# Streaming encoder layer: six first gate products ahead in block one, their order against the first product with t, two more rooms for sums of weights, and the first weight splits behind the columns

## The chip, the core and the metric

The kernel runs on one core of one Trainium2 chip. The core has five engines that each run their own list of instructions strictly in order: TensorE (PE, with its weight loads shown as PEld), VectorE (DVE), ScalarE (ACT), GpSimd (POOL) and SyncE (SP), which only issues transfers here. The metric is device microseconds of one execution; lower is better.

## The reference, cut to what matters

One layer of a streaming encoder on 2048 prompt rows and 64 sample rows, width 1024. The part around the change is the end of the mixers and the feed-forward:

```
x = x + gt1 * (merged @ p['w_o'])
h2 = rms_norm(x, p['norm2_g']) * (1 + sc2) + sh2
gate, up = jnp.split(h2 @ p['w_ffn_in'], 2, axis=-1)
x = x + gt2 * ((jax.nn.silu(gate) * up) @ p['w_ffn_out'])
```

`w_ffn_in` is 1024 x 5632 (2816 gate columns, 2816 up columns), `w_ffn_out` 2816 x 1024, all in f32.

## The kernel before

**Products.** An f32 product is made from three matmuls on halves of the mantissa: each operand is split into a high part (`hi`, a copy on ACT into the type F32R) and a low part (`lo`, source minus high part, on DVE or POOL), and `mm3` adds hi*hi, hi*lo and lo*hi. A split of weights gives a slab `whi`, `wlo`; five slabs are held, and a sixth split waits until TensorE is through with the oldest.

**Blocks.** After attention the tokens are taken in three blocks (`CBLOCKS`): 576, 768 and 768 rows. For each block `s` the kernel merges the mixers, multiplies by `w_o` (tiles `pw`), adds the residual and normalises by tiles of 128 rows (`residual`), turns the rows into columns by transposes on TensorE, and runs the feed-forward. The text calls the block with `s = 0` block one; half of its tokens are 288, so a feed-forward matmul there has 288 columns.

**Seven products instead of eight.** The up part of the feed-forward works on a pair of a gate column and an up column of 128 (`f` from 0 to 21), on two halves of the tokens and two halves of the 1024 inputs. It uses sums of weights, `s1 = u0 + u1`, `s2 = s1 - g0`, `s3 = g0 - u0`, `s4 = g1 - s2` (`Weights.operand`, on POOL, into tiles `ws`, four rooms), and sums of activations, `t1` to `t4`, which `residual` makes on DVE and ACT from the columns `b11`, `b21` (first half of the tokens) and `b12`, `b22` (second half). One product is 12 matmuls: four pieces of 128 inputs, three matmuls each. `up(f)` makes `s3*t3`, `s2*t2`, `s1*t1`, `a22*t4`, `s4*b22`, and the gate's own `a11*b11`, `a12*b21`.

**Products ahead.** `b11` and `b21` need only the first half of the tokens, so they are there before the last token tiles have their columns. For the first `EARLY = 5` gates, `first(f)` (`a11*b11`) and `second(f)` (`a12*b21`, then tanh on ACT and a step on DVE, `silu`) run ahead of `up(0)` and leave both results in tiles `early`. Their weights are whole gate columns with the key `("fi", f * P)`; a split with an odd `f` puts its low part on DVE, with an even one on POOL. The results of one product lie in a PSUM bank; the names `y0`, `z0`, `y1`, `z1` are one bank each. In the last rows of a block the tile before the last (called the fourth token tile in the text, of five in block one) keeps its columns and their sums in `y1` and `z1`; the fifth has other banks.

**Order.** The program hands out instructions with a planner (`Stream`) that adds up an estimated load for each engine, and runs the steps of `residual` as generators (`turns`) between products; a low part of an `up` or `fo` weight goes to DVE if the planned load of POOL is more than `POOL_BEHIND` = 3000 ns ahead of TensorE's. A scheduler then fixes each engine's list: of the instructions that it reckons ready, the one handed out first. `tc.issue_after(ins)` keeps the instructions of its block behind `ins` on the same engine's list. In block one `W.hold` keeps sums and splits of the up weights back until all columns have been handed out. Then come `W.presum()`, which hands out the sums for `f = 0`, `W.begin_last()`, the rest of `turns`, and the products `first(3)`, `second(2)`, `first(4)`, `second(3)`, `second(4)`.

**Rooms and queues.** Raw weights are loaded by SP into rooms `wst` (three), `wup` (one) and `wfo` (two), in the order of `weight_order`; in block one raw columns are shared by all keys that need them (`Weights.first`), and sums go out to DRAM (`sum_d`) for blocks two and three. `token_row` hands out six rooms for whole rows (`x1`, `xn`, later the results `acc`); five of them become `acc` in block one.

## Time and profile before

| | |
|---|---|
| median of 3 runs | 2994.05 us (2993.24 to 2994.75) |
| profiled execution | 2994.99 us, span of the trace 2993.2 us |
| mean granted TensorE clock | 0.995 |
| TensorE busy | 2912.7 us, 97% of the span |
| VectorE, ScalarE, GpSimd busy | 2024.7, 1355.1, 1141.4 us |
| HBM read, written | 476.53 MB, 148.54 MB |
| chain of waits, by engine | PE 80%, DVE 8%, DMA 4%, ACT 2%, POOL 2%, issue 2% |

All lines of the kernel carry one line number (L102, the helper that records every operation), so instructions are told apart by their tiles: `ps<-b` is a product with `b11`, `b21` or `b22`, `ps<-t` one with `t1` to `t4`, `pd` one of the down part, `pw` a bank with the rows of `w_o` or, later, with columns of the last tiles, `xn` the other half of those columns. A row of a timeline has the start in us from the start of the span, the length, engine, operation, result and sources, and in brackets the idle time ahead of it on that engine with what ended it; a row with x3 stands for three instructions in a row. Block one's feed-forward begins near 1312 us, block two's near 1866, block three's near 2495.

### The profile page before, as it was taken

The page shows a single profiled execution, that of the slowest core. Times are in us where ns is not written, and L with a number is a line of the kernel's source. Part 1 is how long each engine was busy: PE and PEld are TensorE (multiplying, and loading weights), DVE is VectorE, ACT ScalarE, POOL GpSimd, SP SyncE. Part 2 cuts the span into 40 slices and gives each one's busy share as a digit, 9 for nine tenths or more (in the row PEclk, how much of TensorE's full clock was granted, in tenths as well). Part 3 has the DMA queues.
Part 4 walks back from the last instruction along what each step waited for, and adds up shares of the span by engine and source line. Part 5 has one row for each costly group of instructions (what it writes and reads, how often), then busy time and mean ns, then how long its engine had stood idle before and what let it go on. Part 6 is the DMA issues. An engine that isn't in the chain of part 4 may idle for free.

```text
span 2993.2 us, 44914 instructions
## 1 busy us (share of the span) xinstructions
PE 2912.7 (97%) x16259; PEld 2593.7 (87%) x16259; DVE 2024.7 (68%) x3596; ACT 1355.1 (45%) x2437; POOL 1141.4 (38%) x734
## 2 busy tenths in 40 slices
PE   7999899999999999989999999999999999999999
PEld 4899777787888788888989889999999999999998
DVE  5887687767857885477677755666666657466666
ACT  3335643662456257464444335534444345344442
POOL 0201310111011102354566433256666741466667
PEclk9999999999999999999999999999999999999999
DMA  8889889888987789885444786423333975333333
GB/s 290 289 284 304 266 288 314 282 255 275 308 280 221 275 246 286 254 293 166 141 141 152 232 269 216 138 89 115 118 101 115 307 248 183 96 93 116 116 102 127
DMA packets 467724, 628.06 MB, mean 210 GB/s; under 512 B 36276, under 2 KB 314664, under 8 KB 467501
## 3 DMA queue, kind: packets, MB, share of 16 engines
q1 hardware_dynamic: 453456, 605.58, 62.5%
q10 hardware_dynamic: 14045, 19.60, 1.9%
q8 instruction: 128, 2.10, 0.3%
q14 instruction: 95, 0.78, 0.1%
HBM read 476.53 MB, written 148.54 MB: 209 GB/s over the span
## 4 chain that ended last, share of the span: by engine, by line
PE 80%; DVE 8%; DMA 4%; ACT 2%; POOL 2%; issue 2%; SPq 1%; ACTq 0%; DVEq 0%; POOLq 0%
PE ps L102 51%; PE pd L102 16%; PE pw L102 5%; DVE y L102 3%; PE sc L102 2%; PE po L102 2%; PE ptp L102 2%; DVE wlo L102 1%; PE pt L102 1%; PE pa L102 1%; ACT whi L102 1%; DMA tg<-g_d 1%; POOL r L102 1%; POOL wlo L102 1%; DVE pw L102 1%
## 5 line engine op out<-in xcount | busy, mean ns | idle before, releaser
L102 PE MATMUL ps<-t,whi 128*128 128x384 f32 (+1 forms) x2112 | 502.5, 322 | 8.8 <-ACT t L102 5.0
L102 POOL TENSOR_TENSOR wlo<-wst,whi 128x1024 fp32r<-128x1024 f32 (+1 forms) x157 | 358.4, 2292 | 287.1 <-ACT whi L102 251.6
L102 ACT ACTIVATE whi<-wst 128x1024 fp32r<-128x1024 f32 (+1 forms) x264 | 257.5, 978 | 331.9 <-PE ps L102 113.8
L102 PE MATMUL ps<-b,whi 128*128 128x384 f32 (+1 forms) x1584 | 381.3, 326 | 6.1 <-DVE early L102 3.3
L102 PEld LDWEIGHTS ps<-t,whi 128*128 128x128 f32 x2112 | 367.7, 188 | 15.8 <-ACT t L102 5.2
L102 DVE SCALAR_TENSOR_TENSOR y<-u,wd,y 128x512 f32<-128x512 f32 (+1 forms) x480 | 369.1, 773 | 6.8
L102 PE MATMUL ps<-hh,whi 128*128 128x512 f32 (+2 forms) x992 | 361.5, 364 | 0.0
L102 DVE TENSOR_TENSOR acc<-acc,pd 128x512 f32<-128x512 f32 (+1 forms) x464 | 311.6, 685 | 66.9 <-PE pd L102 64.1
L102 PE MATMUL ps<-hl,whi 128*128 128x512 f32 (+2 forms) x992 | 345.3, 348 | 0.0
L102 PE MATMUL ps<-hh,wlo 128*128 128x512 f32 (+2 forms) x992 | 345.1, 348 | 0.0
L102 PE MATMUL ps<-t,wlo 128*128 128x384 f32 (+1 forms) x1056 | 339.2, 321 | 0.7 <-POOL wlo L102 0.7
L102 PE MATMUL pd<-whi,hid 128*128 128x512 f32 (+1 forms) x1016 | 325.2, 391 | 0.5 <-DVE acc L102 0.5
L102 PEld LDWEIGHTS ps<-b,whi 128*128 128x128 f32 x1584 | 278.6, 189 | 12.0 <-DVE early L102 4.2
L102 POOL TENSOR_TENSOR r<-t,mhalf 128x1 f32<-128x1 f32 (+3 forms) x68 | 84.1, 1239 | 453.2 <-DVE t L102 448.0
L102 PE MATMUL ps<-b,wlo 128*128 128x384 f32 (+1 forms) x792 | 256.9, 325 | 0.0
L102 ACT ACTIVATE pr<-pr,sm 128x640 f32<-128x640 f32 (+3 forms) x272 | 200.3, 747 | 102.8 <-DVE sm L102 100.5
L102 PEld LDWEIGHTS pd<-whi,hid 128*128 128x128 f32 (+1 forms) x1016 | 185.9, 183 | 45.2 <-DVE acc L102 0.9
L102 PEld LDWEIGHTS ps<-hh,wlo 128*128 128x128 f32 x992 | 186.6, 188 | 21.8
L102 PEld LDWEIGHTS ps<-hh,whi 128*128 128x128 f32 x992 | 187.2, 189 | 18.5 <-issue 1.6
L102 PEld LDWEIGHTS ps<-hl,whi 128*128 128x128 f32 x992 | 187.3, 189 | 15.4 <-issue 1.4
L102 PEld LDWEIGHTS ps<-t,wlo 128*128 128x128 f32 x1056 | 198.2, 188 | 1.9 <-POOL wlo L102 1.3
L102 PE MATMUL pd<-wlo,hid 128*128 128x512 f32 (+1 forms) x508 | 198.5, 391 | 0.0
(225 smaller groups left out, 6173.5 us busy)
## 6 DMA issues: line engine op xcount, KB each, us to landing
whi<-w_din_h SPq DMA_DIRECT2D x72, 512.0 KB, 6.7
wlo<-w_din_l SPq DMA_DIRECT2D x72, 512.0 KB, 7.5
wst<-sum_d SPq DMA_DIRECT2D x132, 256.0 KB, 2.7
wfo<-in_w_ffn_out SPq DMA_DIRECT2D x64, 512.0 KB, 3.3
wmod<-in_w_ada SPq DMA_DIRECT2D x46, 512.0 KB, 7.3
sum_d<-ws SPq DMA_DIRECT2D x88, 256.0 KB, 2.9
wst<-in_w_ffn_in SPq DMA_DIRECT2D x84, 256.0 KB, 3.1
wst<-in_w_in SPq DMA_DIRECT2D x40, 512.0 KB, 9.4
```

What stands on the lines that cost most here:

```text
L102: self.last = f(*args, **kw)
```

## The change

It does five things. `EARLY` becomes a number per block, six in block one and five in the others; the sixth gate's first products use bank `y0` again, and `up(4)` and `up(5)` of block one lose their gate operands. The first product with `t` (`s3*t3` of `f = 0`) is kept behind the last of the products ahead, in all blocks. All splits of `up` weights are kept behind the last column's ACT instruction, in all blocks from the point where the columns are handed out. In block one the first two splits of `up` weights keep their low parts on POOL whatever the planner says (`calm`), and the first two sums take two rooms cut out of one `token_row` (`spare`). Since the operand pairs for `f = 4, 5` now differ between blocks, the weights know block one by a count of blocks rather than by a key's first use.

```diff
--- before.py
+++ after.py
@@ -59,7 +59,7 @@
 TURN_NS = 600.0
 POOL_BEHIND = 3000.0
 KEPT = ("qkv", "in", "fi")
-EARLY = 5
+EARLY = (6, 5, 5)
 
 
 def token_tiles(lo, hi):
@@ -274,7 +274,9 @@
 
         self.staging, self.held, self.reach = staging, held, 0
         self.sum_pool, self.sum_d, self.sums, self.hold, self.landed = None, None, {}, 0, {}
-        self.behind = nullcontext
+        self.behind, self.turn = nullcontext, nullcontext
+
+        self.calm, self.spare = 0, []
 
         self.room, self.leaving = {"wst": 1, "wup": 0, "wfo": 0}, {"wst": 0, "wup": 0, "wfo": 0}
         times, raws = {}, {}
@@ -285,9 +287,11 @@
             self.users.append(0)
             return len(self.items) - 1
 
+        block = 0
         for i, key in enumerate(keys):
             n = times[key] = times.get(key, 0) + 1
-            if key[0] == "up" and n == 1:
+            block += key == ("ca", 0) and n % 2
+            if key[0] == "up" and block == 1:
                 self.first.add(i)
                 cs = [c for f, op in key[1:] for c in self.columns_of(f, op)]
                 for c in cs:
@@ -409,7 +413,7 @@
         made = self.sums.setdefault(f, [])
         while len(made) < int(op[1]):
             j = len(made)
-            t = self.sum_pool.tile([P, 4, P], F32, tag="ws", name="ws", bufs=4)
+            t = self.spare.pop(0) if self.spare else self.sum_pool.tile([P, 4, P], F32, tag="ws", name="ws", bufs=4)
             x, y, e = (
                 lambda: (u[:, :4], u[:, 4:], ALU.add), lambda: (made[0], g[:, :4], ALU.subtract),
                 lambda: (g[:, :4], u[:, :4], ALU.subtract), lambda: (g[:, 4:], made[1], ALU.subtract),
@@ -480,15 +484,17 @@
             parts = [(slice(j, j + n), self.loaded[its[0]][0][:, j : j + n]) for j in range(0, shape[1], n)]
         for c, src in parts:
 
-            late = key[0] in ("up", "fo") and self.stream.load["pool"] - self.stream.load["pe"] > POOL_BEHIND
+            late = not (self.calm and key[0] == "up") and key[0] in ("up", "fo") and self.stream.load["pool"] - self.stream.load["pe"] > POOL_BEHIND
             e, name = (self.dve, "dve") if on_dve or late else (self.gps, "pool")
-            self.act.activation(hi[:, c], src, AF.Copy)
+            with self.turn() if key[0] == "up" else nullcontext():
+                self.act.activation(hi[:, c], src, AF.Copy)
             self.stream.after(name, "act")
             e.tensor_tensor(lo[:, c], src, hi[:, c].bitcast(F32), ALU.subtract)
         if i in self.first:
             its = [self.raws[c] for f, op in key[1:] if op[0] == "a" for c in self.parts_of(f, op)]
         if key[0] == "dn":
             its = [self.raws[*key[:2], key[2] + int(op[1]) - 1] for op in key[3:] if op[0] == "b"]
+        self.calm -= bool(self.calm and key[0] == "up")
         for j in its:
             self.drop(j, name)
         if key[0] == "dn" and key[3] == "b11":
@@ -553,11 +559,11 @@
 ORDER = [(b, st) for b in range(4) for st in ("q", 0, "k", 1, "v", 2, 3, "g")]
 
 
-def up_operands(f):
-
-
-
-    ops = (["s2", "s3", "s1"] if f else ["s3", "s2", "s1"]) + ["a22"] + ["a12"] * (f >= EARLY) + ["a11"] * (EARLY <= f + 1 < NF) + ["s4"]
+def up_operands(s, f):
+
+
+
+    ops = (["s2", "s3", "s1"] if f else ["s3", "s2", "s1"]) + ["a22"] + ["a12"] * (f >= EARLY[s]) + ["a11"] * (EARLY[s] <= f + 1 < NF) + ["s4"]
     return [(f + (op == "a11"), op) for op in ops]
 
 
@@ -596,9 +602,9 @@
         for _ in range(2):
             yield from (("ca", c) for c in range(KT))
             yield from (("wo", k) for k in range(KT))
-        yield from (("fi", f * P) for f in range(EARLY))
+        yield from (("fi", f * P) for f in range(EARLY[s]))
         for f in range(0, NF, 2):
-            ops = up_operands(f) + up_operands(f + 1)
+            ops = up_operands(s, f) + up_operands(s, f + 1)
             for j in range(0, len(ops), 2):
                 yield ("up", *ops[j : j + 2])
                 if f >= 2 and seven(s, f - 2):
@@ -1856,8 +1862,9 @@
                 turns.add(gens[i])
 
         hid = [wk.tile([P, 2, 2, CW], F32R, tag="m0", name="hid"), None]
-        early = wk.tile([P, 2 * EARLY - 2, CW // 2], F32, tag="m1", name="early")
-        early = [[early[:, 2 * f + j] for j in range(2)] for f in range(EARLY - 1)]
+        ahead = EARLY[s]
+        early = wk.tile([P, 2 * ahead - 2, half], F32, tag="m1", name="early")
+        early = [[early[:, 2 * f + j] for j in range(2)] for f in range(ahead - 1)]
         early.append([piece("t2", "early") for _ in range(2)])
         acc = [None] * len(tiles)
 
@@ -1903,7 +1910,7 @@
 
 
             def __init__(self, f0):
-                self.ops = [(e, op) for f in (f0, f0 + 1) for e, op in up_operands(f)]
+                self.ops = [(e, op) for f in (f0, f0 + 1) for e, op in up_operands(s, f)]
                 self.at = 0
 
             def use(self, f, op):
@@ -1925,7 +1932,7 @@
                 product(ps, ops.use(e, op), b, first, last)
                 ops.done()
 
-            if f < EARLY:
+            if f < ahead:
                 s1, c1 = (t[:, :half] for t in early[f])
                 y = bank(Y[f % 2 * 2])
             else:
@@ -1935,12 +1942,13 @@
             z = None
             if not f:
                 z = bank("z0")
-                step(z, "s3", "t3", True, False)
-            step(y, "s2", "t2", f < EARLY, False)
+                with tc.issue_after(ahead_done):
+                    step(z, "s3", "t3", True, False)
+            step(y, "s2", "t2", f < ahead, False)
             if late:
                 rest(*late.pop())
             u2 = piece("t1", "u2")[:, :half]
-            keep = (lambda dst, ps: plus(dst, ps, s1)) if f < EARLY else copy
+            keep = (lambda dst, ps: plus(dst, ps, s1)) if f < ahead else copy
             keep(u2, y)
             if f:
                 z = bank(Y[f % 2 * 2 + 1])
@@ -1956,13 +1964,13 @@
             step(z, "a22", "t4", False, True)
             plus(z, z, u2)
             next(between, None)
-            if f >= EARLY:
+            if f >= ahead:
                 x = bank("gp")
                 step(x, "a12", "b21", True, True)
                 plus(x, x, s1)
                 silu(c1, x)
             dve.tensor_tensor(z, z, c1, ALU.mult)
-            if EARLY <= f + 1 < NF:
+            if ahead <= f + 1 < NF:
                 ny = bank(Y[(f + 1) % 2 * 2])
                 step(ny, "a11", "b11", True, False, f + 1)
                 begun[f + 1] = ny, piece("t2", "s1")[:, :half]
@@ -1970,7 +1978,7 @@
             next(between, None)
             hidden(f, 0, z)
             step(y, "s4", "b22", False, True)
-            if f < EARLY:
+            if f < ahead:
                 plus(y, y, s1)
             silu(y, y)
             dve.tensor_tensor(y, y, v, ALU.mult)
@@ -2170,7 +2178,7 @@
 
         def first(f):
             w = W.get(("fi", f * P))
-            x = bank(("y0", "z0", "y0", "z1", "y1")[f])
+            x = bank(("y0", "z0", "y0", "z1", "y1", "y0")[f])
             product(x, [t[:, :4] for t in w], "b11", True, False)
             copy(early[f][0][:, :half], x)
             begin[f] = w, x
@@ -2186,13 +2194,23 @@
         while hs["columns"]:
             turns.step(turns.gens[0])
         W.hold = False
+
+        W.turn = lambda ins=act.last.ins: tc.issue_after(ins)
+        if not s:
+            W.calm = 2
+            spare = token_row("ws").rearrange("p (j k n) -> p j k n", j=2, n=P)
+            W.spare = [spare[:, j] for j in range(2)]
         W.presum()
         if not s:
             W.begin_last()
         turns.drain()
-        for step, f in ((first, 3), (second, 2), (first, 4), (second, 3), (second, 4)):
+        steps = [(first, 3), (second, 2), (first, 4), (second, 3), (second, 4)]
+        if ahead > 5:
+            steps[4:] = [(first, 5), (second, 4), (second, 5)]
+        for step, f in steps:
             step(f)
             W.fill()
+        ahead_done = pe.last.ins
         last = last_rows(s)
         for f in range(0, NF, 2):
             ops = Operands(f)
```

## The prediction

> **What bounds the kernel now.** I read the page first, then the chain of waits through the first block's change from the merged rows to the feed-forward, then the stages of that place, then each engine's timeline there.
>
> ```profile
> PE 2912.7 (97%) x16259; PEld 2593.7 (87%) x16259; DVE 2024.7 (68%) x3596; ACT 1355.1 (45%) x2437; POOL 1141.4 (38%) x734
> 1312.00:1328.00 16.00, 12.44 (x90) 11.37 (x88) 9.67 (x21) 12.64 (x28) 8.60 (x8) 1.00 1.04 381
> 1328.00:1333.10 5.10, 0.16 (x2) 0.00 (x0) 5.10 (x11) 4.43 (x9) 0.01 (x1) 0.93 1.04 386
> 1333.10:1339.20 6.10, 6.07 (x25) 6.07 (x26) 6.10 (x10) 2.62 (x5) 3.80 (x3) 0.50 0.57 204
> 1339.20:1350.00 10.80, 9.22 (x70) 8.99 (x69) 10.05 (x15) 5.07 (x10) 6.02 (x5) 1.00 0.58 182
> 1400.00:1730.00 330.00, 327.91 (x2046) 296.46 (x2045) 232.32 (x346) 126.98 (x258) 187.38 (x118) 1.00 0.51 168
> 1866.00:1906.00 40.00, 39.02 (x226) 37.88 (x225) 36.41 (x61) 26.80 (x49) 6.93 (x4) 1.00 0.53 187
> ```
>
> The page's line gives busy time by engine; the other rows are stages (length, then busy time of PE, PEld, DVE, ACT and POOL, the granted clock, DMA share, GB/s). TensorE sets the time: 97% of the span, and 99% in the rest of block one. The hole is 1312 to 1350 us. There PE is idle 3.56 + 4.94 + 0.03 + 1.58 = 10.1 us, and runs six more at clock 0.50. The same place of block two loses 1.0 us; I price block three like it. DVE is without a gap from 1328 to 1339. TensorE's and VectorE's rows tell why:
>
> ```profile
> 1312.14 0.43 PE L102 MATMUL ps<-b,whi 128*128 128x288 f32 x2
> 1320.10 1.47 PE L102 MATMUL pw<-ident,xn 128*128 128x128 f32 x12
> 1323.94 0.53 PE L102 MATMUL ps<-b,whi 128*128 128x288 f32 x2 [2.38 <-DVE early L102]
> 1326.30 0.53 PE L102 MATMUL ps<-b,whi 128*128 128x288 f32 x2 [0.39 <-ACT early L102]
> 1333.13 0.61 PE L102 MATMUL ps<-t,whi 128*128 128x288 f32 x1 [4.98 <-ACT t L102]
> 1333.54 0.68 PE L102 MATMUL ps<-b,whi 128*128 128x288 f32 x2
> 1342.56 0.29 PE L102 MATMUL ps<-t,wlo 128*128 128x288 f32 x1
> 1349.84 0.53 PE L102 MATMUL ps<-t,whi 128*128 128x288 f32 x2 [1.58 <-DVE u L102]
> 1353.11 0.43 PE L102 MATMUL ps<-b,whi 128*128 128x288 f32 x2
> 1354.68 0.30 PE L102 MATMUL ps<-t,wlo 128*128 128x288 f32 x1
> 1322.13 1.08 DVE L102 TENSOR_TENSOR wlo<-ws,whi 128x512 fp32r<-128x512 f32 x1 [5.17 <-ACT whi L102]
> 1325.14 0.68 DVE L102 TENSOR_TENSOR wlo<-ws,whi 128x512 fp32r<-128x512 f32 x1
> 1329.97 0.68 DVE L102 TENSOR_TENSOR wlo<-ws,whi 128x512 fp32r<-128x512 f32 x1
> 1328.73 0.41 DVE L102 TENSOR_SCALAR pw<-pw,A,B 128x128 f32<-128x128 f32 x1
> 1330.57 1.28 DVE L102 TENSOR_TENSOR t<-pw,t 128x512 fp32r<-128x512 f32 x2
> 1332.36 0.69 DVE L102 TENSOR_TENSOR pw<-b,pw 128x512 f32<-128x512 f32 x1
> 1349.34 0.44 DVE L102 TENSOR_TENSOR u<-ps,early 128x288 f32<-128x288 f32 x1
> 1318.25 1.14 ACT L102 ACTIVATE xn<-x,r 128x1024 f32<-128x1024 f32 x1
> 1321.47 1.15 ACT L102 ACTIVATE whi<-ws 128x512 fp32r<-128x512 f32 x2 [2.07 <-POOL ws L102]
> 1322.52 0.69 ACT L102 ACTIVATE tg<-ps 128x288 f32<-128x288 f32 x2
> 1330.74 0.46 ACT L102 ACTIVATE xn<-pw,B,A 128x128 f32<-128x128 f32 x1
> ```
>
> Columns are start, length, instruction, and the idle time ahead of it with what ended it. A product (12 matmuls) is 1354.68 - 1353.11 = 1.57 us. Ten go ahead: six by 1328.1, then PE waits 4.98 us with one matmul of s3·t3 at its head; 1333.54 to 1342.56 are the last four. The head alone is not to blame: the next first product uses bank z1, which the fourth token tile holds until `pw<-b,pw` ends at 1332.36 + 0.69 = 1333.05. Before that PE waited 2.38 us because ACT stood at a split of weight sums (1321.47, waiting for POOL), with two tanh of early gates and all columns queued behind it, and DVE stood 5.17 us behind the same split.
>
> **The change, part by part.**
>
> *First splits behind the columns.* In block one every split of a sum goes behind the last column on ACT (now 1330.74). The two tanh can run when `xn` ends at 1318.25 + 1.14 = 1319.4, their DVE steps by 1321, so the third first product starts right behind the transposes at 1320.10 + 1.47 = 1321.57 instead of 1323.94: **-2.4** (bounds -2.4 and 0). DVE starts on columns then too, near 1321.
>
> *Two splits kept off DVE.* Four low parts (1.08 + 3 x 0.68 = 3.1 us of DVE) go to POOL, at 1.3 us each, by the nearest rows:
>
> ```profile
> 1333.09 1.28 POOL L102 TENSOR_TENSOR ws<-wst 128x512 f32<-128x512 f32 x1 [10.42 <-DVE pw L102]
> 1326.94 0.68 DVE L102 TENSOR_TENSOR b<-xn,b 128x512 fp32r<-128x512 f32 x1
> 1341.11 1.30 POOL L102 TENSOR_TENSOR ws<-wfo,ws 128x512 f32<-128x512 f32 x1 [4.14 <-DVE wlo L102]
> 1341.40 1.56 DVE L102 TENSOR_TENSOR wlo<-ws,whi 128x512 fp32r<-128x512 f32 x1
> ```
>
> POOL has 10.42 us free there, so 5.2 us cost it nothing; f = 1's sums stand behind them on its queue, and without that free time the first t product would be late by up to 5.2 us. The two more rooms fill the rest of the gap: f = 1's first two sums no longer wait for a room until 1333.09. No PE time by itself; what waits next is f = 1's slabs, below.
>
> *Sixth gate, and the order.* Two products (3.14 us) move from f = 4 and 5, where PE is 99% busy, to this place: no work is added on PE. The sixth goes into bank y0, free once the third gate's tanh is done, so it needs no column. The 4.98 us wait is filled by these 3.14 us and by z1 coming free earlier: DVE starts some 2 us earlier and loses the low parts at 1325.14 and 1329.97 (1.2 us), so z1 is free near 1333.05 - 3.3 = 1329.8, when the two are through: **-5.0** (bounds -5.0 and 0). With it goes the slow clock: from 1333.54 on 24 matmuls take 0.24 us instead of 0.13, **-2.7** (bounds -2.7 and 0). [...]
>
> New waits: the sixth product for y0's tanh and addition, and its second half for a copy; the nearest row is the 0.39 us of 1326.30, the farthest the 2.38. I take **+1.7** for both (bounds +0.4 and +4.8), nearer the short row, since ACT loses its splits. Behind these on PE stand all the t products.
>
> *What is late next: DVE.* It has two tiles of column work: 6 columns of 0.3 (0.41 alone, the ends overlap) and 22 steps of 0.6 (two in 1.28), together 15.1 us. Counted from 1321 there are besides six gate steps of 0.4 (as long as `u`), two low parts of the sixth gate (turn odd, so DVE: 1.3), the six low parts of f = 0's s4 and f = 1 (4.5 at up to 1.56), and gaps of 1: `u` starts near 1345.5 instead of 1349.34. PE ends its 12 products near 1336.8, has s3, s2 and f = 1's s2 and s3 as cover (6.3 us, to 1343.1), and then waits about 2.5 instead of 1.58: **+0.9** (bounds -1.6, all low parts on POOL, and +4.7, none of f = 1's products ready for cover).
>
> *At nothing.* The sixth gate's column is loaded twice (another 512 KB) and stands ahead of f = 0's in the queue; f = 0's sums may start one load later:
>
> ```profile
> 1315.87 1.15 SPq L375 DMA_DIRECT2D wst<-in_w_ffn_in  x1
> 1338.19 0.38 SPq L375 DMA_DIRECT2D wst<-in_w_ffn_in  x1
> 1311.87 5.16 DMA wst<-in_w_ffn_in
> ```
>
> A landing 5.16 us after its issue at 1315.87 gives three sums by 1325, split in high and low by 1327.5; PE asks for them at 1336.8, so 9 us of other products hide it; without that cover each late load costs its 4 to 10 us. In blocks two and three the product order is already the forced one, and only ACT's order changes:
>
> ```profile
> 1877.54 1.05 ACT L102 ACTIVATE whi<-wst 128x1024 fp32r<-128x1024 f32 x1
> 1884.87 0.44 ACT L102 ACTIVATE pw<-pw,B,A 128x128 f32<-128x128 f32 x1
> 1890.24 0.52 PE L102 MATMUL ps<-t,whi 128*128 128x384 f32 x2
> ```
>
> The split of 1877.54 moves behind 1884.87; its slab is the second that PE takes, after 1894. I take 0 for each block (bounds -1.0, its whole idle time, and +1.5).
>
> Sum: -2.4 - 5.0 - 2.7 + 1.7 + 0.9 = **-7.5 us**. The profiled execution took 2994.99 (span 2993.2 and 1.79 around it), so 2987.5; it lies 0.94 above the median of 2994.05, against which I say **2986.5**.
>
> **Rivals.**
>
> 1. *DVE isn't late.* Planner and scheduler keep the later low parts off DVE or behind `u`: the last two positive terms are -1.6 and +0.4 instead of +0.9 and +1.7, so -11.3: about 2983. For: POOL's gap; against: the planner gives low parts to DVE whenever POOL is reckoned 3 us behind, and the four forced ones put it there.
>
> 2. *PE stands at the fourth gate.* If the scheduler issues the fourth gate's product ahead of the sixth's, PE stands from 1325.1 to 1329.8 for z1 (4.7 us), the clock drops again (2.7), and nothing covers it: -7.5 + 2.7 + 3 = -1.8, the time 2992. For: program order; against: the scheduler already passed that product by for s3·t3.
>
> 3. *POOL holds up DVE.* The low part at 1341.40 took 1.56 instead of 0.68 while POOL ran. With POOL now busy under the columns, the two `b<-xn,b` (0.68 alone) and the sixth gate's low parts can each lose 0.9: 3.5 us on the engine that is late next, 2990. [...]
>
> 4. *Given back at the first product down.*
>
> ```profile
> 1360.70 2.41 POOL L102 TENSOR_TENSOR wlo<-wfo,whi 128x1024 fp32r<-128x1024 f32 x1 [6.17 <-ACT whi L102]
> 1363.19 0.39 PE L102 MATMUL pd<-whi,hid 128*64 128x512 f32 x1
> ```
>
> The second down weight is split at 1363.11, just in time. If that chain keeps its time, all 7.5 us are lost there: 2994. Against: it hangs on a slab that PE frees, and moves with PE.
>
> 5. *Slower: f = 0's column arrives too late.* One mechanism: the sixth gate's load and its slab push f = 0's raw column down the load queue. Its weights are ready 6.2 us after landing (three sums of 1.28, a high part of 0.6, a low part and its queue of 1.8). From a landing at 1330.6 each us is lost, and the gain is gone at 1338. In the slot issued at 1338.19 it lands at 1343.4, PE starts t at 1349.6 instead of 1336.8, 12.8 late, and cold (2.7): 2986.5 + 15.5 = 3002. For: DMA is full there (share 1.04). Against: that slot is 22 us behind the one at 1315.87, and only one load more stands ahead.
>
> **Chances.** Forecast 0.52 (its own range 2983.5 to 2989.5), rivals 0.17, 0.08, 0.06, 0.06 and 0.11. About 0.2% (6 us, below 2988.1) is what a measurement can tell: three quarters of the forecast and the first rival are beyond it, 0.56 faster; the rest of the forecast and rivals two to four, 0.33, same; the last, 0.11, slower. The range, 2982 to 2995, leaves out the last rival and the edge of the first.
>
> **What would show it.** Right: in block one twelve products with b without the 4.98 us wait, clock 1.00 throughout, no `whi<-ws` on ACT ahead of the last column, the first four `wlo<-ws` on POOL, `u` near 1345. Wrong: a new PE wait of over 3 us ahead of the fourth gate or of `u`, a wait for `whi<-ws` by the first t product, or a first `pd` still at 1363.

## The result and the profile after

| | before | after |
|---|---|---|
| median of 20 runs, us | 2994.17 (2987.60 to 2998.46) | 3001.07 (2994.21 to 3005.35) |
| ratio after to before, 95% interval | | 1.0019 (1.0014 to 1.0025) |
| profiled execution (its span), us | 2994.99 (2993.2) | 2995.12 (2993.3) |
| block one, two, three, us | 417.10, 492.40, 497.82 | 418.96, 493.98, 498.99 |

The change costs 0.19% of 2994 us: 5.7 us, between 4.2 and 7.5 (the medians in the table lie 6.9 apart). The forecast was 2986.5, with 2982 to 2995 as its range.

The two profiled spans are equal by chance: block one's first product with b starts at 1312.14 us before and at 1307.67 after, and TensorE's work ahead of that place is the same in both. Over all profiles of this study it started anywhere from 1307.67 to 1320.46. So spans are of no use here, and I compare stretches. A block's stretch runs from its first product with b to the first product of the next block (in block three, to the end), and splits at the first product with t and at the first product down. These are stages of block one, then all of block two (length; busy PE, PEld, DVE, ACT, POOL; granted clock; DMA share; GB/s), of the kernel before:

```profile
1312.14:1333.13 20.99, 12.46 (x89) 11.26 (x87) 14.66 (x31) 16.93 (x36) 8.64 (x9) 0.98 1.04 382
1333.13:1363.19 30.06, 28.48 (x192) 28.20 (x193) 27.19 (x42) 13.61 (x26) 15.97 (x11) 0.90 0.60 191
1363.19:1729.24 366.05, 362.77 (x2246) 326.29 (x2245) 259.93 (x391) 144.02 (x290) 205.72 (x131) 1.00 0.52 170
1866.13:2358.53 492.40, 491.04 (x2585) 459.47 (x2584) 319.07 (x524) 219.55 (x372) 291.77 (x175) 1.00 0.40 127
```

The same stages of the changed kernel:

```profile
1307.67:1340.25 32.58, 23.66 (x162) 22.44 (x160) 26.23 (x47) 23.37 (x50) 19.17 (x16) 0.90 0.88 314
1340.25:1362.69 22.44, 19.88 (x146) 19.13 (x145) 20.85 (x33) 9.14 (x17) 12.70 (x9) 1.00 0.71 236
1362.69:1726.63 363.94, 359.53 (x2223) 323.26 (x2221) 254.96 (x385) 142.00 (x283) 197.24 (x127) 1.00 0.51 168
1862.82:2356.80 493.98, 491.29 (x2585) 459.49 (x2584) 320.65 (x524) 218.90 (x372) 290.68 (x175) 1.00 0.39 126
```

The first product down comes 55.02 us after the start instead of 51.05. Of these 3.97 us, 3.14 are the sixth gate's two products, moved ahead; the rest of the block gives back only 2.11. Block two's busy PE is the same to 0.25 us and the stretch is 1.58 longer: PE waits there. In sum the three blocks are 1.86 + 1.58 + 1.17 = 4.6 us longer; the two merges between blocks are 273.75 us before and 273.70 after.

TensorE, VectorE and ScalarE in block one of the changed kernel (timeline; start, length, instruction, idle time ahead of it and what ended that):

```profile
1313.78 1.14 ACT L102 ACTIVATE whi<-wup 128x512 fp32r<-128x512 f32 x2
1314.43 3.42 DVE L102 TENSOR_TENSOR wlo<-wup,whi 128x512 fp32r<-128x512 f32 x2 [1.95 <-ACT whi L102]
1317.77 0.41 DVE L102 TENSOR_SCALAR pw<-pw,A,B 128x128 f32<-128x128 f32 x1
1318.59 0.53 PE L102 MATMUL ps<-b,whi 128*128 128x288 f32 x2 [1.60 <-DVE early L102]
1319.38 0.42 DVE L102 TENSOR_SCALAR pw<-pw,A,B 128x128 f32<-128x128 f32 x1 [0.15 <-ACT pw L102]
1320.54 0.42 DVE L102 TENSOR_SCALAR pw<-pw,A,B 128x128 f32<-128x128 f32 x1 [0.38 <-ACT pw L102]
1321.26 0.70 DVE L102 TENSOR_TENSOR pw<-xn,pw 128x512 f32<-128x512 f32 x1 [0.30 <-ACT xn L102]
1325.80 0.69 DVE L102 TENSOR_TENSOR pw<-pw,b 128x512 f32<-128x512 f32 x1
1327.59 0.69 DVE L102 TENSOR_TENSOR pw<-pw,b 128x512 f32<-128x512 f32 x1
1328.19 0.69 DVE L102 TENSOR_TENSOR pw<-b,pw 128x512 f32<-128x512 f32 x1
1329.02 0.82 PE L102 MATMUL ps<-b,whi 128*128 128x288 f32 x2 [6.25 <-DVE pw L102]
1343.95 0.53 PE L102 MATMUL ps<-t,whi 128*128 128x288 f32 x2 [1.70 <-DVE early L102]
```

The 4.98 us wait for the first t is gone, and a wait of 6.25 us stands in its place. It belongs to the fourth gate's first product, whose bank z1 the column steps give back with `pw<-b,pw`, at 1328.19 + 0.69 = 1328.88. That is 21.2 us into the block; before it was 1333.05 - 1312.14 = 20.9. The bank came no earlier, and the sixth gate's two products, which should have filled the time, are queued behind the one that waits. VectorE has no gap in those 6.25 us. Ahead of the first column step it now makes the sixth gate's low parts, 3.42 us for two where one took 0.68 (the row at 1329.97 of the kernel before); ahead of `pw<-b,pw` it makes two steps of the other tile (`pw<-pw,b` at 1325.80 and 1327.59) that stood behind it before. These two steps take the place of the two low parts that are gone from here (1325.14 and 1329.97 before), and three waits for ScalarE's columns come on top (0.15, 0.38 and 0.30 us in the rows above). So VectorE needs 11.1 us from its first column step to z1 (1317.77 to 1328.88), against 9.9 before (to 1333.05, from this row):

```profile
1323.13 0.41 DVE L102 TENSOR_SCALAR pw<-pw,A,B 128x128 f32<-128x128 f32 x1
```

Block two, changed kernel:

```profile
1882.42 1.07 ACT L102 ACTIVATE whi<-wst 128x1024 fp32r<-128x1024 f32 x1
1884.21 1.09 ACT L102 ACTIVATE whi<-wst 128x1024 fp32r<-128x1024 f32 x1
1885.16 0.52 ACT L102 ACTIVATE early<-ps 128x384 f32<-128x384 f32 x1
1885.73 0.62 PE L102 MATMUL ps<-b,whi 128*128 128x384 f32 x2 [0.76 <-ACT early L102]
1887.14 2.41 POOL L102 TENSOR_TENSOR wlo<-wup,whi 128x1024 fp32r<-128x1024 f32 x1 [12.02 <-ACT whi L102]
1887.67 2.96 DVE L102 TENSOR_TENSOR wlo<-wst,whi 128x1024 fp32r<-128x1024 f32 x1
1890.56 1.28 DVE L102 TENSOR_TENSOR t<-pw,t 128x512 fp32r<-128x512 f32 x2
1891.29 0.45 PE L102 MATMUL ps<-t,whi 128*128 128x384 f32 x1 [0.91 <-DVE t L102]
```

And the kernel before at the same place:

```profile
1889.85 1.22 DVE L102 TENSOR_TENSOR wlo<-wup,whi 128x1024 fp32r<-128x1024 f32 x1
1889.89 3.45 POOL L102 TENSOR_TENSOR wlo<-wst,whi 128x1024 fp32r<-128x1024 f32 x1 [11.44 <-ACT whi L102]
1893.39 0.44 PE L102 MATMUL ps<-t,wlo 128*128 128x384 f32 x1 [0.35 <-POOL wlo L102]
```

The split that stood 1877.54 - 1866.13 = 11.4 us into the block before is now 1882.42 - 1862.82 = 19.6 us into it, and with the one behind it (2.2 us together) it stands ahead of the copy at 1885.16, for which a first product with b waits 0.76 us. Behind the splits come the low parts, and VectorE's now meets GpSimd's: GpSimd began first and VectorE's took 2.96 us instead of 1.22, with the steps that make t behind it and 0.91 us of waiting on TensorE. Before, VectorE began 0.04 us ahead and GpSimd's took 3.45 instead of 2.41, at the cost of a wait of 0.35 us. The two new waits less that one are 1.3 of the 1.58 us. In both pairs the low part that began second is the longer one, by 1.74 us on VectorE and 1.04 on GpSimd.

### The profile page after: what moved, and what is told of

Read it like the earlier page. It is cut to its first block, busy times and chain, and to the rows that moved or that the text cites. A ratio compares the mean times of both kernels' runs of the same rounds, so it can differ in the third digit from the quotient of the medians.

```text
span 2993.3 us, 44903 instructions
## 1 busy us (share of the span) xinstructions
PE 2911.2 (97%) x16259; PEld 2592.7 (87%) x16259; DVE 2028.1 (68%) x3597; ACT 1352.5 (45%) x2435; POOL 1138.0 (38%) x735
## 4 chain that ended last, share of the span: by engine, by line
PE 47%; DVE 2%; ACT 1%; DMA 1%; issue 1%; POOL 0%; SPq 0%; ACTq 0%; DVEq 0%; POOLq 0%
PE ps L102 28%; PE pd L102 14%; PE pw L102 4%; DVE wlo L102 1%; DVE pw L102 1%; DVE t L102 0%; ACT whi L102 0%; DMA cin<-o_d 0%; DMA tg<-g_d 0%; DVE ps L102 0%; PE pt L102 0%; ACT xn L102 0%; DMA wst<-in_w_conv_out 0%; DVE b L102 0%; DMA sum_d<-ws 0%
## 5 line engine op out<-in xcount | busy, mean ns | idle before, releaser
L102 POOL TENSOR_TENSOR wlo<-wst,whi 128x1024 fp32r<-128x1024 f32 (+1 forms) x165 | 372.3, 2265 | 330.3 <-ACT whi L102 329.1
L102 PEld LDWEIGHTS ps<-b,whi 128*128 128x128 f32 x1584 | 277.5, 189 | 20.7 <-ACT whi L102 6.4
```

What stands on the lines that cost most here:

```text
L102: self.last = f(*args, **kw)
```

## The experiments

Each but before_again is the changed kernel, with the edit shown. All stretches are from its profile, in us; a run without a ratio was executed once:

| run | block one | two | three | ratio to before, 95% interval |
|---|---|---|---|---|
| before_again | 417.17 | 492.34 | 497.86 | |
| after_again | 420.03 | 493.96 | 499.09 | |
| turn_one | 419.85 | 492.38 | 497.48 | 1.0012 (1.0003 to 1.0020) |
| no_turn | 418.29 | 492.39 | 497.67 | |
| five_ahead | 415.85 | 493.99 | 498.93 | 1.0006 (0.9997 to 1.0014) |
| five_turn_one | 417.06 | 492.39 | 497.40 | 0.9991 (0.9982 to 1.0000) |
| five_again | 415.89 | 492.41 | 497.43 | |
| five_no_turn | 416.27 | 492.39 | 497.38 | 0.9996 (0.9987 to 1.0005) |
| sixth_first | 418.81 | 493.95 | 499.04 | 1.0009 (1.0000 to 1.0018) |
| sixth_z0 | 416.63 | 492.41 | 497.46 | 0.9993 (0.9984 to 1.0002) |
| sixth_z0_no_turn | 415.88 | 492.39 | 497.45 | 1.0005 (0.9997 to 1.0014) |
| six_pool | 420.71 | 493.97 | 499.08 | 1.0020 (1.0011 to 1.0029) |
| fourth_z0 | 421.63 | 496.51 | 500.95 | 1.0028 (1.0018 to 1.0038) |
| five_calm4 | 418.29 | 492.39 | 497.39 | 1.0002 (0.9993 to 1.0010) |
| fourth_z0_calm4 | 420.77 | 496.55 | 500.90 | |
| no_order | 419.53 | 493.97 | 499.03 | |
| no_calm | 420.80 | 493.99 | 499.08 | |
| no_spare | 419.21 | 493.93 | 499.43 | |

**How far one kernel scatters.** The kernel before, the changed kernel, and five_turn_one, the one with five gates of which more is said below, each profiled again.

> The kernel before once more, profiled, to learn how far the stretches of one program differ between executions. Theory (the loss is made in the three feed-forward blocks, the rest is chance): from the first product with b to the block's end 417.1, 492.4 and 497.8 us again, each within 0.5; the time up to the first product of block one may differ by several us. Rival (the stretches themselves scatter by 1 to 2 us, so the differences read off one profile mean nothing): a block's stretch differs by 1 us or more.

> The changed kernel once more. If the stretches belong to the program, block one takes 418.96 us give or take 0.3, blocks two and three 493.98 and 498.99; if block one scatters with what its loads meet, it differs by up to 1.2 us while the other two stay.

> Five gates with the turn in block one alone, once more. If block one scatters, it lies anywhere from 415.8 to 417.1 us, with a different set of waits behind 30 us; if it belongs to the program, 417.06 give or take 0.3.

Blocks two and three repeat within 0.1 us, block one of the kernel before within 0.07. But block one of the changed kernel took 418.96 and 420.03, with five gates 417.06 and 415.89. In the changed kernel most of that is the slow clock behind the wait. Windows of the changed kernel and of its second profile, behind the same wait:

```profile
1329.02:1332.62 3.60, 3.60 (x15) 3.52 (x16) 3.60 (x7) 2.21 (x5) 3.60 (x4) 0.50 0.05 19
```

```profile
1342.01:1347.81 5.80, 5.80 (x24) 5.71 (x25) 5.76 (x10) 2.28 (x5) 4.68 (x4) 0.51 0.28 87
```

In 3.60 us at half speed (15 matmuls, where the next 2.40 us have 20) 1.8 us are lost, in 5.80 us 2.9: the difference of 1.1 us is as much as lies between 418.96 and 420.03. With five gates the clock is only a part: the first product down comes 50.07 us into the block in five_turn_one and 49.50 in five_again, so 0.6 of their 1.17 us arise behind it, at full clock. And five_ahead, whose program is the same in block one, lost the clock a second time (for 3.3 us of work from 1343.96 on) and took 415.85 all the same. So one profile of block one can be off by 1.2 us. Below I name runs by the slow stretch behind their first long wait, "short" (up to 4 us) or "long" (over 5), and compare like with like: the changed kernel has 418.96 short, 420.03 and (turn_one, same waits in block one) 419.85 long, 419.94 on the mean. In the kernel before, slow stretches of 6.1 and 2.8 us made no difference, so against it a figure of block one is good to about 1 us. Like five_ahead, the runs five_calm4, six_pool, sixth_first and the two of fourth_z0 have a second slow stretch further on, 3.3 to 3.4 us of work, which these names leave out.

**The order behind the last column in blocks two and three.**

```diff
-        W.turn = lambda ins=act.last.ins: tc.issue_after(ins)
+        W.turn = (lambda ins=act.last.ins: tc.issue_after(ins)) if not s else nullcontext
```

> The change with the splits kept behind the columns in block one alone. Theory (that order costs blocks two and three 1.6 and 1.2 us): their stretches fall from 494.0 and 499.0 back to 492.4 and 497.8, block one stays at 419.0, the time is 2.7 us below the changed kernel, ratio to before 1.0010. Rival (blocks two and three are slower for another reason, the forced order of the first t product or what they inherit from block one): the stretches stay, ratio 1.0019.

Both blocks go back: 493.98 to 492.38 and 498.99 to 497.48. GpSimd's and VectorE's low parts again meet in the old order, and the 0.91 us wait is gone:

```profile
1893.39 1.22 DVE L102 TENSOR_TENSOR wlo<-wst,whi 128x1024 fp32r<-128x1024 f32 x1
1893.42 3.44 POOL L102 TENSOR_TENSOR wlo<-wup,whi 128x1024 fp32r<-128x1024 f32 x1 [11.44 <-ACT whi L102]
```

Every run with this order in blocks two and three has the high values, every run without it the low ones, except the two of fourth_z0, which use other banks there. It costs 1.6 and 1.5 us.

**The sixth gate taken out.**

```diff
-EARLY = (6, 5, 5)
+EARLY = (5, 5, 5)
```

> The change with five gates ahead in block one too (forced order, rooms, splits behind the columns and two splits on POOL stay). Theory (the sixth gate's products don't fill the wait for bank z1, its low part holds up VectorE at 1314, and it gives 1.7 us back at y0): block one's stretch is no longer than with six, 416 to 419. Rival (the sixth gate's two products are worth the 3.1 us that they take away later, and the other parts cost more): block one's stretch grows to 421 or more. Blocks two and three stay at 494.0 and 499.0 by both.

With turn_one's edit beside it:

> Five gates ahead, not six, and the first splits of the transposed weights behind the last column in block one alone; the rest of the change as it is. If the parts add up: block one as with five gates ahead (415.85 us from its first product with b to its end, where before took 417.10), blocks two and three as with the turn in block one alone (492.38 and 497.48 against 492.40 and 497.82 of before): 1.25 + 0.0 + 0.3 = 1.6 us less than before in all, a ratio of 0.9995. If the parts do not add up, because the load on VectorE in blocks two and three depends on what block one leaves, the three stretches together are no shorter than the 1407.3 us of before and the ratio is 1.0000 or above.

Block one is 415.85 and 415.89 with a short slow stretch, 417.06 with a long one. Against six gates that is 3.1 us less (418.96) and 2.9 less (419.94), and the longest with five lies 1.9 us below the shortest with six. Five gates, first column step, the step that frees z1, and the product that waits for it (five_turn_one, block from 1312.23):

```profile
1320.47 0.42 DVE L102 TENSOR_SCALAR pw<-pw,A,B 128x128 f32<-128x128 f32 x1 [3.43 <-PE pw L102]
1330.51 0.69 DVE L102 TENSOR_TENSOR pw<-b,pw 128x512 f32<-128x512 f32 x1
1331.26 0.85 PE L102 MATMUL ps<-b,whi 128*128 128x288 f32 x2 [5.54 <-DVE pw L102]
```

z1 is free 1331.20 - 1312.23 = 19.0 us into the block, 2.2 earlier than with six, and nothing stands behind the wait that does not have to. As to time, five_turn_one lies 0.09% below the kernel before with an interval that ends at no difference: not a gain that these runs can hold for certain.

**The sixth gate's products handed out earlier, in y0, then in z0.** The first:

```diff
-        yield from (("fi", f * P) for f in range(EARLY[s]))
+        yield from (("fi", f * P) for f in ((0, 1, 2, 5, 3, 4) if EARLY[s] > 5 else range(EARLY[s])))
...
-            steps[4:] = [(first, 5), (second, 4), (second, 5)]
+            steps = [(second, 2), (first, 5), (second, 5), (first, 3), (first, 4), (second, 3), (second, 4)]
```

> The change with the sixth gate's slab and both its products handed out ahead of the fourth gate's. Theory (TensorE stands 6.25 us at the fourth gate's first product for bank z1 with the sixth's two products behind it): these 3.1 us of work fill the wait, which falls to 2 to 3 us, the clock stays at 1.00, block one's stretch falls from 419.0 to 414 to 415.5. Rival (VectorE's column work sets when the first t products can run, so a wait only moves): the wait shows up again ahead of s2 t2 or of u, and block one's stretch stays within 1 us of 419.0.

The wait moved on to the sixth's own bank (sixth_first: ScalarE's tanh of the third gate, VectorE's step behind it, the sixth's first product):

```profile
1330.41 0.41 ACT L102 ACTIVATE tg<-ps 128x288 f32<-128x288 f32 x1
1333.65 0.44 DVE L102 SCALAR_TENSOR_TENSOR early<-tg,ps 128x288 f32<-128x288 f32 x1
1334.15 0.85 PE L102 MATMUL ps<-b,whi 128*128 128x288 f32 x2 [5.00 <-DVE early L102]
```

The tanh is done at 1330.82; VectorE does its half 2.8 us later, behind column steps. No column lies in y0, but it waits for the columns all the same. Block one took 418.81, as the rival of the expectation had it. It did wait less, 13.3 us in all against 15.9 in the changed kernel, but it ran 9.5 us of its work at half clock (the second stretch from 1353.88 on) against 3.6, which takes the gain back. The second run also has the first one's order of the weights and the order of turn_one:

```diff
-            x = bank(("y0", "z0", "y0", "z1", "y1", "y0")[f])
+            x = bank(("y0", "z0", "y0", "z1", "y1", "z0")[f])
...
-            steps[4:] = [(first, 5), (second, 4), (second, 5)]
+            steps = [(first, 5), (second, 2), (second, 5), (first, 3), (first, 4), (second, 3), (second, 4)]
```

> The sixth gate's two products handed out ahead of the fourth's, into bank z0 (free since the second gate's step) where the run with the sixth's products first used y0; the turn in block one alone. If the sixth gate's products cost because they stand behind a wait for a bank that VectorE gives back late, they now fill the wait at some 21 us after the block's first product with b: of the 6.25 us (fourth gate's bank) or 5.00 us (y0) about 2 are left, and block one takes 414 to 416 us, with blocks two and three at 492.4 and 497.5. If VectorE's queue behind the column steps is what sets the order of all banks, the wait turns up at the next product in the list, and block one takes 418 to 420 us as in the two runs with six gates.

416.63 (short): 2.3 us less than the changed kernel, though the sixth gate's two products, splits and low parts are all there. The wait for z1 is what is left behind the products that now fill it:

```profile
1330.08 0.54 PE L102 MATMUL ps<-b,whi 128*128 128x288 f32 x2 [3.90 <-DVE pw L102]
```

It lies above the 414 to 416 us expected and below the rival's 418 to 420: of the wait 3.90 us were left, not about 2, and all waits of block one together are 13.8 us, near the 13.4 of the kernel before. z1 comes free 20.7 us into the block in both runs, so the gain does not come from there.

**Bank or VectorE?** The fourth and fifth gates in banks free of columns, the sixth in z1, with turn_one's edit beside it:

```diff
-            x = bank(("y0", "z0", "y0", "z1", "y1", "y0")[f])
+            x = bank(("y0", "z0", "y0", "z0", "y0", "z1")[f])
...
-            steps[4:] = [(first, 5), (second, 4), (second, 5)]
+            steps = [(first, 3), (second, 2), (second, 3), (first, 4), (second, 4), (first, 5), (second, 5)]
```

> Six gates in their own order, but the fourth's sums in bank z0 (free since the second gate's step) and the fifth's in y0, so that only the sixth's needs z1, which the columns give back last; order of halves: fourth first, third second, fourth second, fifth first and second, sixth first and second; the turn in block one alone. If the wait of 5 to 6 us for z1 was a matter of which bank the next product has in the list, four more products run inside it, the waits ahead of the first product with t (5.64 us with the sixth in z0, 6.69 with five gates) fall under 3 us and block one takes 413 to 414.5 us. If VectorE's steps, queued behind the columns, set the pace, the wait turns up at y0 or at the first steps with t, all the waits of block one together stay at 12 to 14 us as in the kernel before (13.4), with five gates (13.5) and with the sixth in z0 (13.8), and block one takes 416 to 418 us.

421.63, and all waits of block one 16.5 us. (The table of banks holds for blocks two and three too, which took 4.1 and 3.5 us more than in turn_one; the ratio has that in it.) The third gate's tanh was done at 1326.57 and VectorE's half of it at 1336.49, so y0 came free 4.6 us later than the columns' bank, which a product had from 1331.93 on:

```profile
1326.16 0.41 ACT L102 ACTIVATE tg<-ps 128x288 f32<-128x288 f32 x1 [0.62 <-PE ps L102]
1331.93 0.85 PE L102 MATMUL ps<-b,whi 128*128 128x288 f32 x2 [4.23 <-DVE pw L102]
1336.05 0.44 DVE L102 SCALAR_TENSOR_TENSOR early<-tg,ps 128x288 f32<-128x288 f32 x1
```

The expectation of 413 to 414.5 us was wrong, and so was the size its rival named (416 to 418 us, with waits of 12 to 14). The rival's mechanism is what the rows show: a bank free of columns comes back no sooner when the step that frees it stands behind column steps in VectorE's queue. Taking more low parts off VectorE, first in five_turn_one, then in fourth_z0:

```diff
-            W.calm = 2
+            W.calm = 4
```

> Five gates, the turn in block one alone, and the low parts of the first four pairs of transposed weights kept on GpSimd, not two. With two, VectorE made four to six low parts of sums between the column steps, 5.7 us from 1335.59 to 1344.1 us of that run. If VectorE's queue is the bound at the first products with t, the waits after the first product with t (2.37 us there) and at the next gate (1.40 and 0.30) go and block one takes 414.5 to 416 us. If it only moves work to GpSimd, whose low parts take twice as long, the first product down or the next pair waits and block one takes 417 us or more.

> Both of the edits before together. If banks and VectorE's load are two separate costs, block one is shorter than either alone, by what the one gave below 417.06 added to what the other gave. If both are the same bound, it is within 1 us of the better one.

418.29 against 417.06 (both long) with five gates: 1.2 us more, though five_calm4 has a second slow stretch of 3.4 us, so that the low parts on GpSimd cost this much is not shown. With the banks above, 420.77 against 421.63. Neither is a gain that these runs can show, alone or together.

**The sixth gate's low parts alone on GpSimd.**

```diff
-        on_dve = key[0] == "in" or key[0] == "qkv" and (passing or key[1]) or turn % 2
+        on_dve = key[0] == "in" or key[0] == "qkv" and (passing or key[1]) or turn % 2 and key != ("fi", 5 * P)
```

> The change with one thing else: the two low parts of the sixth gate's column (3.42 us on VectorE from 1314.43 us, ahead of the first column step) on GpSimd; every other instruction stands in the same order on every engine. If these two are what keeps z1, the first column step comes 1.5 to 2 us earlier, the wait of 1.60 us ahead of the third gate goes, the fourth gate's product starts 19 to 20 us after the block's first product with b instead of 21.35, and block one takes 416.5 to 417.5 us. If the place of the products on TensorE is the cause, z1 comes free at 21 us as before and block one takes 418.5 us or more; and if GpSimd's queue is the tighter one, the first products with t wait for weights 2 us or more longer, with the same end.

I had taken these 3.42 us for the cause; the run says that moving them to GpSimd does not help (block from 1315.22):

```profile
1323.49 0.42 DVE L102 TENSOR_SCALAR pw<-pw,A,B 128x128 f32<-128x128 f32 x1 [3.45 <-PE pw L102]
1328.24 1.81 DVE L102 TENSOR_TENSOR b<-xn,b 128x512 fp32r<-128x512 f32 x1
1335.09 0.69 DVE L102 TENSOR_TENSOR pw<-b,pw 128x512 f32<-128x512 f32 x1
1335.92 0.82 PE L102 MATMUL ps<-b,whi 128*128 128x288 f32 x2 [7.38 <-DVE pw L102]
```

The first column step comes 8.3 us into the block, as with five gates, 1.8 earlier than in the changed kernel, and the 1.60 us wait ahead of the third gate is gone. But z1 comes free at 20.6, only 0.65 earlier: VectorE needs 12.3 us from the first column step to that point (11.1 in the changed kernel, 10.7 with five gates, 9.9 before). One step beside GpSimd's work took 1.81 instead of 0.68. TensorE, done sooner with what it could do, waits 7.38 us, and block one took 420.71 (with a second slow stretch), the time 0.2% above before as with the change whole.

**The other parts, one at a time.** Without the forced order of the first product with t; without the low parts kept on GpSimd; without the two rooms; without the order behind the last column in any block:

```diff
-                with tc.issue_after(ahead_done):
-                    step(z, "s3", "t3", True, False)
+                step(z, "s3", "t3", True, False)
```

```diff
-            W.calm = 2
+            W.calm = 0
```

```diff
-            W.spare = [spare[:, j] for j in range(2)]
+            W.spare = []
```

```diff
-        W.turn = lambda ins=act.last.ins: tc.issue_after(ins)
```

> The change without the order that puts the first product with t behind the last product ahead. If the wait for the fourth gate's bank sets the time of the stretch, nothing with t is ready much earlier and block one takes 418.96 us give or take 0.5 (as with the change whole). If the forced order itself costs, a product with t goes into the 6.25 us wait and block one comes to 416 us or less.

> The change with the planner free to put the low parts of the first two pairs of transposed weights on VectorE in block one, as in the kernel before. If keeping them on GpSimd is worth something, VectorE's queue ahead of the second gate's steps is some 3 us longer, the wait for the fourth gate's bank or the one after it is longer by 1 to 3 us, and block one takes 420 to 422 us. If VectorE has slack there, 418.96 give or take 0.5.

> The change without the two more rooms for sums of weights. If the rooms do something for the time, the sums of the second pair start later and the first products with t or the next gate wait 1 to 3 us longer: block one 420 to 422 us. If the sums have slack, as was said in the forecast, 418.96 give or take 0.5.

> The change without the order that keeps the high parts of transposed weights behind the last column, in all three blocks; six gates, rooms and low parts as in the change. Blocks two and three go back to 492.4 and 497.5 us on either theory. In block one: if the order gives what the forecast said (the tanh of the early gates 2.4 us sooner), without it the wait ahead of the third gate comes back at 2.4 us or more and block one takes 420 us or more; if the gain is eaten by the sixth gate's own low part anyway, block one stays at 418 to 420 us.

The forced order costs nothing that one profile can show (419.53 with 5.2 us of slow clock). The rooms give nothing (419.21 and 418.96, both short). The low parts on GpSimd look worth 0.9 us (420.80 against 419.94, long), which is within the scatter of one profile. The order behind the columns seems to cost in block one as well: 418.29 without it, 1.7 us less (both long), but by a single profile. The third gate's wait did not come back at 2.4: it is 1.59 with or without. What went is part of the wait behind it, now 3.47 us and for a gate's step on VectorE:

```profile
1331.15 0.85 PE L102 MATMUL ps<-b,whi 128*128 128x288 f32 x2 [3.47 <-DVE early L102]
```

The last two runs leave this order out beside five gates, and beside the sixth gate in z0 (edits as above):

> Five gates and no order behind the last column; the two more rooms, the low parts kept on GpSimd and the order of the first product with t as in the change. With the order in block one, five gates took 417.06 and 415.89 us there. If the order is a loss whatever stands behind the columns' bank, block one comes to 415 us; if it is a loss only together with the sixth gate's own split ahead of the columns, 416 to 417 us; if it gives the tanh of the early gates their 2.4 us, 418 us. Blocks two and three 492.4 and 497.4 on each. In time a ratio of 0.9985 to 0.9995 to the kernel before.

> The sixth gate in bank z0 ahead of the fourth, and no order behind the last column. With the order in block one it took 416.63 us. If the order is a loss in itself, 415 to 416 us; if not, 416.6 give or take 1.1 (one kernel's scatter from execution to execution), or up to 419 if splits on ScalarE hold up the early gates again. Blocks two and three 492.4 and 497.4.

416.27 against 417.06 (long), 415.88 against 416.63 (short): 0.8 us less each time, which is again within the scatter: 416.27 lies between the 415.85 and 417.06 of five gates with the order. The times do not bear it out either: 0.9996 where five_turn_one has 0.9991, 1.0005 where sixth_z0 has 0.9993, with intervals that overlap. So whether this order costs anything in block one stays open; no run shows a gain from it there. No version is faster than the kernel before by more than its interval: five_no_turn has 1.3 us less over the three blocks (1406.04 to 1407.32) and a ratio of 0.9996 (0.9987 to 1.0005).

## Why the prediction was wrong

The sign that the prediction named for being wrong came: a new wait of over 3 us ahead of the fourth gate. By the steps of block one:

- *First splits behind the columns, -2.4:* the wait of 2.38 became 1.60, -0.8. With five gates or with six_pool it is gone: the sixth gate's low parts, which the forecast counted after 1321 at 1.3 us, stood ahead of the first column step and took 3.42. With five gates the order did what was said of it (1.37 us of wait without it, none with it), and block one was no shorter for it.
- *Sixth gate, and the order, -5.0: the step that failed.* It had the 3.14 us of the sixth's products fill the wait, and z1 free near 1329.8, or 17.7 us into the block. z1 was free at 21.2, and the sixth's products stood behind the fourth's, as the program hands them out. 4.98 became 6.25, +1.3. The 3.5 us between 17.7 and 21.2 are VectorE's, in three parts of about 1.2 us each. It began its column steps 0.9 us earlier in the block, not 2.1, because of the sixth gate's low parts; the two low parts taken off it were made up for by two steps of the other tile ahead of the one that counts; and it waited three times for ScalarE's columns, 0.83 us together, with the overlap of its steps lost each time (behind one another, at 1327.59 and 1328.19, steps of 0.69 us start 0.60 apart). Why the scheduler put the two steps there I can't tell from the runs. That the place of the products is half of the matter is shown by sixth_z0: handed out ahead of the fourth's, into a bank that is free, they took 2.3 us off block one with z1 only 0.5 us earlier.
- *Slow clock, -2.7:* it stayed, 3.6 us of it in one profile and 5.8 in the other, 1.8 to 2.9 us lost, so -1.3 to -0.2 against 6.1 us, or 3.1 lost, in the profile before. The term was also priced too high: before_again ran 3.3 us less of its work at half speed than the first profile, and block one took the same time.
- *Waits for y0, +1.7:* right in sum, but by luck, since the sixth's product was not the one that waited: 0.28 in place of 0.39, and 1.70 at 1343.95, where the first pair's product waits for the sixth gate's step.
- *VectorE late at `u`, +0.9:* that wait (1.58) went; others for `v` came, 0.79 in the same pair and 1.40 in place of 0.61 in the next. About nothing. With the short slow stretch the steps so far come to +0.8 of the +1.9; the rest lies in smaller waits and in matmul time that no run takes apart.
- *Blocks two and three, 0 each (bounds -1.0 and +1.5):* +1.58 and +1.17, shown by turn_one to be the order behind the last column. I had looked at the one slab's due time and not at the copy and the low parts that its split would now stand beside.

The second rival, TensorE at the fourth gate, was the mechanism of block one: it named a wait of 4.7 us and the clock, and had 2992, because it kept the -2.4 whole and nothing for blocks two and three. The third, GpSimd holding up VectorE, came true for the sixth gate's low parts, which it named: 3.42 us against the 1.3 of the forecast. The two `b<-xn,b`, which it named too, kept their time in the changed kernel (0.68 and 0.74); block two, where it happened again, it did not name. The first (VectorE not late) had the wait at `u` gone, which came, but its gain of 11.3 did not. The fourth did not happen: TensorE has no wait ahead of the first product down. The fifth, late weights, did not: no product with t waited for a weight of f = 0.

The sum as measured: block one +1.9 to +2.9 (418.96 and 420.03 against 417.10), blocks two and three +2.8, together 4.6 to 5.7 us, which is the 5.7 of the times. Taking one part away from the whole, the sixth gate costs about 3 us in block one, and the order behind the columns 3.1 us in the other two and between nothing and 1.7 in block one; what is left without both is no measurable gain.

## What to carry to other kernels

Work put ahead of a wait fills it only if nothing that it is queued behind waits for the same engine: the sixth gate's 3.14 us left a wait of 6.25 us where they stood behind the fourth gate's products, and one of 3.90 us ahead of them, in z0. Ask for every bank, buffer or operand of the filler which engine gives it back, and count that engine's queue up to that step, the other tiles' steps too. An order that is set for one stage and applied to all is to be priced in each: here its clear cost, 1.6 and 1.5 us, lay in the two stages where nothing had been wrong. And profile one kernel more than once before a difference of 1 us is given a cause: here the same program took 418.96 and 420.03 us for block one.

## What the runs showed of the hardware

The granted clock fell to 0.50 for 3.4 us (sixth_z0_no_turn), 6.8 (five_again) or 10.2 (after_again), and the fall did not come at the start of the wait. Windows of five_again, from 1.5 us into its wait, which began at 1325.30, to the end of the slow stretch (... stands for windows left out):

```profile
1326.80:1327.30 0.50, 0.00 (x0) 0.00 (x0) 0.50 (x2) 0.00 (x0) 0.00 (x0) 1.00 1.12 409
1327.30:1327.80 0.50, 0.00 (x0) 0.00 (x0) 0.50 (x2) 0.14 (x1) 0.00 (x0) 0.57 1.06 408
...
1334.00:1334.40 0.40, 0.40 (x3) 0.40 (x3) 0.40 (x1) 0.28 (x1) 0.40 (x1) 0.76 0.07 22
```

By the shares at half speed, the clock fell near 1327.4, 2.1 us into the wait, and came back near 1334.2, 6.8 us later; in sixth_z0_no_turn it fell 2.6 us into a wait of 2.89 and came back after 3.4. From the start of the wait to the fall it was 1.9 us in after_again and 4.2 in the kernel before. So a wait's price in clock was not fixed: the same kernel lost 1.8 or 2.9 us. Nor was there one long wait each time: the kernel before, far ahead of block one, lost the clock near 188.9 us, behind waits of 0.89 and 0.61 us and 0.2 us into one of 0.65. And one and the same wait of 2.64 us on TensorE, for GpSimd's `s`, was followed by 0.50 in the changed kernel (from 271.06 to 274.47, 1.6 us after its end) and by 1.00 in the kernel before (from its end at 272.37 to 276.00 and on).
